# The block inverse of a chunked RWKV-7 mixer: both directions taken stage by stage, its copies on two engines

## The chip, the cores and the metric

One core of a Trainium2 chip runs the whole program. The metric is device time in microseconds (us) of one execution; a stated time is the median of several runs.

## The reference

One layer of a hybrid backbone over 256 latent and 256 context tokens, width 2048. The part that matters here is the bidirectional RWKV-7 mixer (16 heads of 64), beside the gates that the layer computes from the same projection:

```
def rwkv7_scan(s0, r, decay, k, v, kk, a, reverse):
    def step(S, inp):
        r_t, w_t, k_t, v_t, kk_t, a_t = inp
        sa = jnp.einsum('bhvk,bhk->bhv', S, kk_t)
        S = (S * w_t[:, :, None, :] - sa[..., None] * (kk_t * a_t)[:, :, None, :]
             + v_t[..., None] * k_t[:, :, None, :])
        return S, jnp.einsum('bhvk,bhk->bhv', S, r_t)
...
def merge_branches(p_gate, y_rwkv, y_diff, w_pa, w_pb, w_out):
    gates = jax.nn.sigmoid(p_gate.reshape(*p_gate.shape[:-1], 2, D_MODEL))
    mixed = gates[..., 0, :] * (y_rwkv @ w_pa) + gates[..., 1, :] * (y_diff @ w_pb)
    return mixed @ w_out
```

A mixture of experts (32 experts, two for each token) follows.

## The kernel before

The scan is done in chunks of 64 tokens: 8 chunks (4 of context, 4 of latent tokens) in each of two directions. Within a chunk the recurrence is a triangular system, so each chunk, direction and head needs the inverse of a 64x64 unit triangular matrix A. The heads are worked through in four quarters, q0 to q3, each with two head pairs (o = 0 and 1). For a quarter and head pair, A holds 2 directions x 8 chunks x 2 heads = 32 matrices; index m = 0 to 15 is the forward direction, 16 to 31 the backward one.

`inverse` works by blocks of 32. The two diagonal blocks of all 64 matrices of a quarter are inverted together on VectorE, row by row (L1426, L1428, 31 steps). Two transposes then give ZT (L1431) and Z (L1433). The off-diagonal block is completed by two 32x32 products for each matrix on TensorE: ph = A x ZT (L1442), evacuated into H, which is the same tile as ZT (L1444); then pz = H x Z (L1451), evacuated back into A (L1453). The inverted diagonal blocks are copied from Z into A as well (L1454). A head pair's operands lie in 64 partitions of its own, so the ph products of o = 0 and of o = 1 stand at two different positions of the engine's array (`tile_position`), each 32 rows by 32 columns; so do the pz products.

Behind it, `deltas` multiplies with the finished A: pW (L1243, alternating between the two head pairs, both into one PSUM bank) and pu (L1251, one head pair in each bank), four times, then pG (L1268), which alternates over head pairs and heads, four positions, with a bank for each head pair; then the chain of states pS.

The rest of the layer is a second stream of work: projections as products of 128x128 weights with 256 tokens (L490, the operands split into a high part whi by ScalarE, L968, and a low part wlo, L969, by VectorE, or by GpSimd for those parts that are recorded while an inverse is being recorded), and the sums of the conditioning vector's projection, ada (L614). In this part of the program these are mostly the gates' products. The generators of the mixer yield a number of microseconds; `interleave` then advances the second stream by that many, times 0.444. This gives the order in which instructions are recorded, which is their priority; a scheduler then places them on the engines by readiness and priority, and each engine runs its list in order.

Of the kernel before, what the change touches and what calls it, by code (L numbers as in the profile page):

```python
# [200 lines left out]
class Body:  # L201
# [1205 lines left out]
    def rows(self, o, i):  # L1407
        return slice((1 - o) * 64 + 32 * i, (1 - o) * 64 + 32 * i + 32)

    def inverse(self, As):  # L1410

        nc, tl, pst = self.nc, self.rwt, self.pst
        NB = 2 * NC * 2
        Av = [A.rearrange("p d c h t -> p (d c h) t") for A in As]

        na = tl("na", [P, 32, 32], tag="b0")
        z = tl("z", [P, 32, 32], tag="b1")
        prod = tl("prod", [P, 32, 32], tag="b2")
        rows = self.rows
        nc.vector.transpose(na.rearrange("b s t -> b t s"), self.dg16.rearrange("p d n t -> p t (d n)"))  # L1420
        yield 1.5
        nc.gpsimd.memset(z, 0.0)
        nc.gpsimd.memset(z.rearrange("b s t -> b (s t)")[:, ::33], 1.0)
        for s in range(30, -1, -1):
            n = 31 - s
            nc.vector.tensor_tensor(prod[:, :n, :n], z[:, s + 1:, s + 1:], na[:, s, s + 1:].unsqueeze(1).to_broadcast([P, n, n]),  # L1426
                                    ALU.mult)
            nc.vector.tensor_reduce(z[:, s + 1:, s], prod[:, :n, :n], AX.X, ALU.add)  # L1428
            yield 0.25 + n * n * 0.002
        ZT = H = tl("ZT", [P, NB, 32], tag="b3")  # L1430
        nc.vector.transpose(ZT.rearrange("p n s -> p s n"), z.rearrange("b t s -> b s t"))  # L1431
        Z = self.rb.tile([P, NB, 32], F32, tag="s", name="Z")
        nc.vector.transpose(Z.rearrange("p n t -> p t n"), z)  # L1433
        yield 3.077

        for g in range(2):
            ph = [pst("ph") for _ in range(2)]
            for o in range(2):
                r0, r1 = rows(o, 0), rows(o, 1)
                for n in range(16):  # L1440
                    m = g * 16 + n
                    nc.tensor.matmul(ph[o][r1, n * 32:n * 32 + 32], Av[o][r0, m, 32:64], ZT[r0, m, :],  # L1442
                                     start=True, stop=True, tile_position=(r0.start, r1.start))
                nc.scalar.copy(H[r1, g * 16:g * 16 + 16], ph[o][r1, :].rearrange("p (n t) -> p n t", n=16))  # L1444
            yield 0.7
            pz = [pst("pz") for _ in range(2)]
            for o in range(2):
                r0, r1 = rows(o, 0), rows(o, 1)
                for n in range(16):
                    m = g * 16 + n  # L1450
                    nc.tensor.matmul(pz[o][r0, n * 32:n * 32 + 32], H[r1, m, :], Z[r1, m, :],  # L1451
                                     start=True, stop=True, tile_position=(r1.start, r0.start))
                nc.scalar.copy(Av[o][r0, g * 16:g * 16 + 16, 32:64], pz[o][r0, :].rearrange("p (n t) -> p n t", n=16))  # L1453
                nc.scalar.copy(Av[o][rows(o, g), :, 32 * g:32 * g + 32], Z[rows(o, g)])  # L1454
            yield 0.7

    def pst(self, name):
        return self.ps.tile([P, 512], F32, tag="ps", name=name)
# [517 lines left out]
```

## Time and profile before

| | |
|---|---|
| median of 3 runs | 2495.0 us (2490.64, 2495.00, 2501.33) |
| the profiled execution | 2500.59 us, span 2499.0 us |
| mean granted TensorE clock | 0.971 of full speed |
| TensorE (PE) busy | 2337.1 us, 94% |
| VectorE (DVE) busy | 1203.3 us, 48% |
| ScalarE (ACT) busy | 796.1 us, 32% |
| GpSimd (POOL) busy | 218.5 us, 9% |
| the four quarters of the mixer | about 730 to 1340 us of the span |
| the experts | about 1600 us to the end, DMA share 0.99 |

The span is the time from the first to the last instruction of the profiled execution. A busy engine need not be a fast one: the granted clock says at which share of 2.4 GHz TensorE ran, 1.00 or 0.50 (1.2 GHz) at any moment, something between as a mean.

### The profile page before, as it was taken

The page shows a single profiled execution, that of the slowest core. Times are in us where ns is not written, and L with a number is a line of the kernel's source. Part 1 is how long each engine was busy: PE and PEld are TensorE (multiplying, and loading weights), DVE is VectorE, ACT ScalarE, POOL GpSimd, SP SyncE. Part 2 cuts the span into 40 slices and gives each one's busy share as a digit, 9 for nine tenths or more (in the row PEclk, how much of TensorE's full clock was granted, in tenths as well). Part 3 has the DMA queues.
Part 4 walks back from the last instruction along what each step waited for, and adds up shares of the span by engine and source line. Part 5 has one row for each costly group of instructions (what it writes and reads, how often), then busy time and mean ns, then how long its engine had stood idle before and what let it go on. Part 6 is the DMA issues. An engine that isn't in the chain of part 4 may idle for free.

```text
span 2499.0 us, 45067 instructions
## 1 busy us (share of the span) xinstructions
PE 2337.1 (94%) x18419; PEld 1647.7 (66%) x18419; DVE 1203.3 (48%) x2234; ACT 796.1 (32%) x1479; POOL 218.5 (9%) x279
## 2 busy tenths in 40 slices
PE   6999989899999999999999898999999999999997
PEld 3799987788998787787899877444334443343342
DVE  3355578768656574685755665222222222222223
ACT  3322345455345564565644343000000000000000
POOL 0110012112113332201000000000000000000000
PEclk9999999999998997999899999999999999999999
DMA  9977764557754242353347896899999999999997
GB/s 348 329 246 233 239 218 137 166 176 245 236 172 136 78 129 94 114 174 85 122 130 233 255 333 235 323 427 428 427 427 427 428 428 427 428 427 427 428 427 325
DMA packets 205476, 691.46 MB, mean 277 GB/s; under 512 B 31768, under 2 KB 69328, under 8 KB 179792
## 3 DMA queue, kind: packets, MB, share of 16 engines
q1 hardware_dynamic: 205264, 688.53, 73.8%
q8 instruction: 146, 2.39, 0.4%
q14 instruction: 66, 0.54, 0.1%
HBM read 666.66 MB, written 21.78 MB: 275 GB/s over the span
## 4 chain that ended last, share of the span: by engine, by line
PE 54%; DMA 17%; DVE 8%; issue 4%; ACT 3%; POOL 2%; SPq 0%; DVEq 0%; POOLq 0%; ACTq 0%
PE acc L490 12%; DMA xd<-in_exp_w_dram 10%; PE pa L1822 9%; PE po L1856 9%; PE pt L1754 5%; PE acc L815 4%; PE pt L1873 3%; DMA raw<-in_ws_dram 2%; DMA w<-in_exp_w_dram 2%; PE pc L1132 1%; DVE prod L1426 1%; PE pu L1251 1%; PE pz L1451 1%; PE ph L1442 1%; DVE wlo L969 1%
## 5 line engine op out<-in xcount | busy, mean ns | idle before, releaser
L968 ACT CAST whi<-raw 128x512 fp32r<-128x512 f32 (+1 forms) x463 | 280.2, 614 | 318.8 <-PE acc L490 144.5
L969 DVE TENSOR_TENSOR wlo<-raw,whi 128x512 fp32r<-128x512 f32 (+1 forms) x420 | 289.2, 702 | 89.5 <-ACT whi L968 83.5
L490 PE MATMUL acc<-xr,whi 128*128 128x256 f32 (+1 forms) x1248 | 273.4, 297 | 0.0
L490 PE MATMUL acc<-xd,whi 128*128 128x256 f32 (+1 forms) x1248 | 267.9, 292 | 0.7 <-ACT whi L968 0.7
L1822 PE MATMUL pa<-w,hg 128*64 128x512 f32 x1024 | 226.5, 594 | 16.2 <-DMA w<-in_exp_w_dram 12.8
L1856 PE MATMUL po<-w,hT 128*64 128x512 f32 (+1 forms) x1040 | 230.8, 590 | 1.5 <-DMA w<-in_exp_w_dram 0.7
L490 PEld LDWEIGHTS acc<-xr,whi 128*128 128x128 f32 (+1 forms) x1248 | 212.3, 198 | 19.6 <-issue 18.0
L490 PEld LDWEIGHTS acc<-xd,whi 128*128 128x128 f32 (+1 forms) x1248 | 207.2, 193 | 18.7 <-issue 13.6
L1769 DVE TENSOR_TENSOR hm<-hm,pa 128x512 f32<-128x512 f32 x16 | 11.0, 688 | 405.9 <-PE pa L1822 405.9
L490 PE MATMUL acc<-xr,wlo 128*128 128x256 f32 (+1 forms) x624 | 184.5, 296 | 4.7 <-DVE wlo L969 4.1
L490 PE MATMUL acc<-xd,wlo 128*128 128x256 f32 (+1 forms) x624 | 181.9, 291 | 1.1 <-DVE wlo L969 1.1
L607 DVE SCALAR_TENSOR_TENSOR ada<-raw,cs,ada 128x512 f32<-128x512 f32 x180 | 137.1, 769 | 95.2 <-DMA raw<-in_ws_dram 94.8
L1822 PEld LDWEIGHTS pa<-w,hg 128*64 128x64 f32 x1024 | 71.8, 137 | 165.6 <-issue 132.8
L1856 PEld LDWEIGHTS po<-w,hT 128*64 128x64 f32 x1040 | 70.4, 137 | 133.8 <-issue 127.3
L1880 DVE TENSOR_TENSOR acc<-acc,pt 128x512 f32<-128x512 f32 x112 | 75.3, 682 | 152.4 <-PE pt L1873 152.4
L1863 ACT ACTIVATE ohl<-po,gc 128x512 fp32r<-128x512 f32 x60 | 41.3, 688 | 296.6 <-PE po L1856 296.6
L490 PEld LDWEIGHTS acc<-xr,wlo 128*128 128x128 f32 (+1 forms) x624 | 123.6, 198 | 8.9 <-DVE wlo L969 5.7
L1754 PE MATMUL pt<-pe,xa 128*128 128x128 f32 x1024 | 123.6, 279 | 5.9 <-DVE hg L1756 5.2
L1822 PE MATMUL pa<-xd,hg 128*64 128x512 f32 x496 | 113.1, 598 | 16.1 <-DMA xd<-in_exp_w_dram 16.1
L1822 PE MATMUL pa<-xr,hg 128*64 128x512 f32 x496 | 113.1, 598 | 15.4 <-DMA xr<-in_exp_w_dram 15.4
L1754 PEld LDWEIGHTS pt<-pe,xa 128*128 128x128 f32 x1024 | 118.6, 194 | 12.1 <-DVE hg L1756 8.8
L490 PEld LDWEIGHTS acc<-xd,wlo 128*128 128x128 f32 (+1 forms) x624 | 120.3, 193 | 4.2 <-DVE wlo L969 1.5
(393 smaller groups left out, 4205.7 us busy)
## 6 DMA issues: line engine op xcount, KB each, us to landing
w<-in_exp_w_dram SPq DMA_DIRECT2D x128, 2048.0 KB
raw<-in_ws_dram SPq DMA_DIRECT2D x703, 256.0 KB
xr<-in_exp_w_dram SPq DMA_DIRECT2D x31, 2048.0 KB
xd<-in_exp_w_dram SPq DMA_DIRECT2D x31, 2048.0 KB
xt<-in_ws_dram SPq DMA_DIRECT2D x39, 512.0 KB
raw<-in_ws_dram SPq DMA_DIRECT2D x25, 512.0 KB
g<-gate SPq DMA_DIRECT2D x48, 128.0 KB
kvr<-own SPq DMA_DIRECT2D x16, 256.0 KB
```

The lines of the kernel that those rows point to most:

```text
L490: m = nc.tensor.matmul(acc[j][:M, n * T:n * T + T], a[:, k2, j * M:(j + 1) * M], (rl if i == 1 else rh)[k], start=(k == 0 and i == 0 and s ...
L607: nc.vector.scalar_tensor_tensor(a, raw, c, a, ALU.mult, ALU.add)
L815: nc.tensor.matmul(acc[i], a[:, i * P:(i + 1) * P], b[:, k - k0, :], start=(k == 0 and q == 0), stop=(k == KT - 1 and q == 2))
L968: self.nc.scalar.copy(hi, src)
L969: (eng or self.nc.vector).tensor_tensor(lo, src, f32(hi), ALU.subtract)
L1132: nc.tensor.matmul(pc[h][:, c * C:c * C + C], flat(kq[d][H2[h], c]), pr[d][H2[h], c], start=True, stop=True, tile_position=(h * 64, 0))
L1754: nc.tensor.matmul(p[:, k * P:(k + 1) * P], xa[:, i, (k4 + k) * P:(k4 + k + 1) * P], pe[:, i, :], start=(i == 0), stop=(i == 1))
L1822: nc.tensor.matmul(a[es_, :], hg[:, k4 + k, es_], w[:, e, k, :], start=(k4 + k == 0), stop=(k4 + k == KT - 1), tile_position=(0, e * 64))
L1856: nc.tensor.matmul(o[es_, :], hT[:, f, es_], w[:, e, f, hs], start=(f == 0), stop=(f == 3), tile_position=(0, e * 64))
L1863: nc.scalar.activation(oh[:, n, hs], o, AF.Copy, scale=gc)
L1873: nc.tensor.matmul(y, one[:, i * P:(i + 1) * P], o, start=(h == 0), stop=(h == 1))
L1880: nc.vector.tensor_tensor(acc[:, i, os], acc[:, i, os], y, ALU.add)
```

## The change

For each quarter, all copies of the diagonal blocks are recorded ahead of the products, half on ScalarE (o = 0) and half on VectorE (o = 1). Then ph is made for both directions (g = 0, 1) with the two head pairs alternating, each direction in a bank for both head pairs; then pz in the same way. The evacuations are split between the two engines like the copies. The yields become 6.0 and four times 1.4, where they were 3.077 and four times 0.7.

```diff
-        yield 3.077
-
+        yield 6.0
+
+        for o in range(2):
+            for i in range(2):
+                rs = rows(o, i)
+                (nc.vector.tensor_copy if o else nc.scalar.copy)(Av[o][rs, :, 32 * i:32 * i + 32], Z[rs])
+        ph = [pst("ph") for _ in range(2)]
         for g in range(2):
-            ph = [pst("ph") for _ in range(2)]
+            for n in range(16):
+                m = g * 16 + n
+                for o in range(2):
+                    r0, r1 = rows(o, 0), rows(o, 1)
+                    nc.tensor.matmul(ph[g][r1, n * 32:n * 32 + 32], Av[o][r0, m, 32:64], ZT[r0, m, :],
+                                     start=True, stop=True, tile_position=(r0.start, r1.start))
             for o in range(2):
-                r0, r1 = rows(o, 0), rows(o, 1)
-                for n in range(16):
-                    m = g * 16 + n
-                    nc.tensor.matmul(ph[o][r1, n * 32:n * 32 + 32], Av[o][r0, m, 32:64], ZT[r0, m, :],
-                                     start=True, stop=True, tile_position=(r0.start, r1.start))
-                nc.scalar.copy(H[r1, g * 16:g * 16 + 16], ph[o][r1, :].rearrange("p (n t) -> p n t", n=16))
-            yield 0.7
-            pz = [pst("pz") for _ in range(2)]
+                r1 = rows(o, 1)
+                (nc.vector.tensor_copy if o else nc.scalar.copy)(H[r1, g * 16:g * 16 + 16],
+                                                                 ph[g][r1, :].rearrange("p (n t) -> p n t", n=16))
+            yield 1.4
+        pz = [pst("pz") for _ in range(2)]
+        for g in range(2):
+            for n in range(16):
+                m = g * 16 + n
+                for o in range(2):
+                    r0, r1 = rows(o, 0), rows(o, 1)
+                    nc.tensor.matmul(pz[g][r0, n * 32:n * 32 + 32], H[r1, m, :], Z[r1, m, :],
+                                     start=True, stop=True, tile_position=(r1.start, r0.start))
             for o in range(2):
-                r0, r1 = rows(o, 0), rows(o, 1)
-                for n in range(16):
-                    m = g * 16 + n
-                    nc.tensor.matmul(pz[o][r0, n * 32:n * 32 + 32], H[r1, m, :], Z[r1, m, :],
-                                     start=True, stop=True, tile_position=(r1.start, r0.start))
-                nc.scalar.copy(Av[o][r0, g * 16:g * 16 + 16, 32:64], pz[o][r0, :].rearrange("p (n t) -> p n t", n=16))
-                nc.scalar.copy(Av[o][rows(o, g), :, 32 * g:32 * g + 32], Z[rows(o, g)])
-            yield 0.7
+                r0 = rows(o, 0)
+                (nc.vector.tensor_copy if o else nc.scalar.copy)(Av[o][r0, g * 16:g * 16 + 16, 32:64],
+                                                                 pz[g][r0, :].rearrange("p (n t) -> p n t", n=16))
+            yield 1.4
```

The scheduler's order shows what becomes of it on TensorE in q0, from the last gates' product ahead of ph. Here x32 counts 32 instructions in a row; xr, xd and whi, wlo are operands of the gates' products. Before:

```order
L490 MATMUL acc<-xr,wlo 128x256
L1442 MATMUL ph<-ZT,A 32x32 x32
L490 MATMUL acc<-xr,whi 128x256 x2
L490 MATMUL acc<-xr,wlo 128x256
L614 MATMUL ada<-raw,cs 32x256
L1451 MATMUL pz<-Z,ZT 32x32 x32
L1442 MATMUL ph<-ZT,A 32x32 x32
```

In the change, where ph stands in line 1446 and pz in line 1459:

```order
L490 MATMUL acc<-xr,wlo 128x256
L1446 MATMUL ph<-ZT,A 32x32 x64
L490 MATMUL acc<-xr,whi 128x256
L1459 MATMUL pz<-Z,ZT 32x32
L490 MATMUL acc<-xr,whi 128x256
L490 MATMUL acc<-xr,wlo 128x256
L614 MATMUL ada<-raw,cs 32x256 x2
```

The 64 ph instructions of both directions now follow each other; the gates' products ahead of them are as many as before, 2649 since the program's start.

The end of the same place in q0, on TensorE, from the last pz to the finished A's first uses pW and pu. Before:

```order
L1451 MATMUL pz<-Z,ZT 32x32 x16
L490 MATMUL acc<-xr,whi 128x256
L1451 MATMUL pz<-Z,ZT 32x32 x16
L1243 MATMUL pW<-W,A 64x64
L1251 MATMUL pu<-vu,A 64x64 x8
L490 MATMUL acc<-xr,whi 128x256
L490 MATMUL acc<-xr,wlo 128x256
```

In the change:

```order
L1459 MATMUL pz<-Z,ZT 32x32 x32
L490 MATMUL acc<-xr,wlo 128x256
L1459 MATMUL pz<-Z,ZT 32x32 x31
L1243 MATMUL pW<-W,A 64x64 x16
L1251 MATMUL pu<-vu,A 64x64 x16
L1243 MATMUL pW<-W,A 64x64 x16
L1251 MATMUL pu<-vu,A 64x64 x16
```

Before, a pW, eight pu and then 14 gates' products stood ahead of the other 15 pW; now pW and pu follow pz without products between. In q2 and q3 a pW, eight pu and two or three gates' products still stand ahead of the run.

VectorE in q0, from the last reduction of the inverse (L1428) to the first evacuations of pu and pW. Before:

```order
L1428 TENSOR_REDUCE z<-prod 128x31
L1431 STREAM_TRANSPOSE ZT<-z 128x32x32
L1433 STREAM_TRANSPOSE Z<-z 128x32x32
L1253 COPY vu<-pu 64x512
L1245 COPY W<-pW 128x512
L1253 COPY vu<-pu 64x512 x2
```

In the change, with a wlo of the second stream ahead of the transposes that stood some rows earlier before:

```order
L1428 TENSOR_REDUCE z<-prod 128x31
L969 TENSOR_TENSOR wlo<-raw,whi 128x512
L1431 STREAM_TRANSPOSE ZT<-z 128x32x32
L1433 STREAM_TRANSPOSE Z<-z 128x32x32
L1439 COPY A<-Z 32x32x32 x2
L1450 COPY ZT<-ph 32x512 x2
L1463 COPY A<-pz 32x16x32 x2
L1253 COPY vu<-pu 64x512
```

Six copies come in between the transposes and pu's; ScalarE loses as many.

## Rows read from the trace of the kernel before

**Rows 1.** The page, part 1: busy us, share of the span, instructions.

```profile
PE 2337.1 (94%) x18419; PEld 1647.7 (66%) x18419; DVE 1203.3 (48%) x2234; ACT 796.1 (32%) x1479; POOL 218.5 (9%) x279
```

**Rows 2.** Windows behind each inverse: busy us by engine, clock, DMA share, GB/s.

```profile
core 0: us, PE busy (x) PEld busy (x) DVE busy (x) ACT busy (x) POOL busy (x), PEclk, DMA share, GB/s
...
793.00:821.00 28.00, 27.75 (x342) 23.86 (x343) 2.57 (x3) 10.54 (x15) 4.25 (x4) 0.51 0.17 51
953.00:980.00 27.00, 26.11 (x328) 23.55 (x330) 4.07 (x4) 10.02 (x14) 2.96 (x3) 0.51 0.22 66
1112.00:1131.00 19.00, 19.00 (x312) 17.91 (x312) 4.71 (x8) 10.34 (x16) 0.00 (x0) 0.74 0.19 59
1271.00:1289.00 18.00, 18.00 (x316) 16.63 (x314) 6.58 (x10) 11.36 (x17) 0.31 (x1) 0.79 0.34 104
```

**Rows 3.** Timeline of TensorE, q0: start, duration, records, idle time before.

```profile
793.25 3.35 PE L1442 MATMUL ph<-ZT,A 32*32 32x32 f32 x64 [3.33 <-DVE ZT L1431]
796.53 0.80 PE L490 MATMUL acc<-xr,whi 128*128 128x256 f32 x2
...
813.18 1.91 PE L1251 MATMUL pu<-vu,A 64*64 64x64 f32 x16
...
817.66 1.07 PE L614 MATMUL ada<-raw,cs 128*32 128x256 f32 x4
...
819.60 1.60 PE L1243 MATMUL pW<-W,A 64*64 64x64 f32 x30
```

**Rows 4.** Timeline of TensorE, q1: the first ph and pW's run.

```profile
953.88 3.40 PE L1442 MATMUL ph<-ZT,A 32*32 32x32 f32 x64 [2.75 <-DVE ZT L1431]
...
978.92 1.97 PE L1243 MATMUL pW<-W,A 64*64 64x64 f32 x30
```

**Rows 5.** Timeline of TensorE, q2: the first ph and pW's run.

```profile
1112.51 2.11 PE L1442 MATMUL ph<-ZT,A 32*32 32x32 f32 x64
...
1131.39 1.14 PE L1243 MATMUL pW<-W,A 64*64 64x64 f32 x30
```

**Rows 6.** Timeline of TensorE, q3: products at either clock, ph, pW's run.

```profile
1270.74 0.40 PE L490 MATMUL acc<-xd,whi 128*128 128x256 f32 x2
...
1271.10 0.40 PE L490 MATMUL acc<-xd,whi 128*128 128x256 f32 x2
...
1271.55 2.11 PE L1442 MATMUL ph<-ZT,A 32*32 32x32 f32 x64
1273.59 0.50 PE L490 MATMUL acc<-xd,whi 128*128 128x256 f32 x2
...
1280.37 0.63 PE L490 MATMUL acc<-xd,whi 128*128 128x256 f32 x2
...
1281.01 0.60 PE L490 MATMUL acc<-xd,whi 128*128 128x256 f32 x2
...
1289.10 1.97 PE L1243 MATMUL pW<-W,A 64*64 64x64 f32 x30
```

**Rows 7.** Timeline of TensorE at full clock: products of 64x64 in deltas.

```profile
825.56 1.15 PE L1243 MATMUL pW<-W,A 64*64 64x64 f32 x32
826.54 1.85 PE L1251 MATMUL pu<-vu,A 64*64 64x64 f32 x32
828.32 1.13 PE L1054 MATMUL pw<-lw,w 96*128 96x512 f32 x2
...
1145.14 1.71 PE L1268 MATMUL pG<-kt,W 64*64 64x64 f32 x96
```

**Rows 8.** Timeline of TensorE between q2 and q3, without gates' products.

```profile
1195.14 6.25 PE L1132 MATMUL pc<-P,kq 64*128 64x64 f32 x64
...
1208.33 2.67 PE L1132 MATMUL pc<-P,kq 64*128 64x64 f32 x32
```

**Rows 9.** Timeline of ScalarE in q0 and of VectorE in q2: copies.

```profile
797.24 1.04 ACT L1454 COPY A<-Z 32x1024 f32<-32x1024 f32 x1
...
1128.27 0.69 DVE L1253 COPY vu<-pu 64x512 f32<-64x512 f32 x1 [13.47 <-PE pu L1251]
```

**Rows 10.** Groups of GpSimd: count, busy us, mean ns, idle before.

```profile
L969 POOL TENSOR_TENSOR wlo<-raw,whi 128x512 fp32r<-128x512 f32 x43 | 63.3, 1489 | 113.0 <-ACT whi L968 109.2 <-PE acc L490 2.8 <-PE ada L614 1.0
```

## The prediction

> **What bounds the kernel now.** I read the page's busy times first, then windows for the granted clock, then the timeline of the three engines around each inverse. TensorE is busy for 94% of the span [rows 1] and its program order is fixed, so time goes where TensorE waits or runs slowly. At the end of each of the four inverses (one per quarter, q0 to q3) the reader is to see the second: in the 27 to 28 us behind the inverse's last transposes the granted clock is 0.51 in q0 and q1, which is the 1.2 GHz level nearly throughout, and 0.74 and 0.79 in q2 and q3 [rows 2]. In q0 and q1 TensorE had waited before it, 3.33 and 2.75 us for ZT [rows 3, 4]; in q2 and q3 it did not wait and the clock still fell: the means say 10 of 19 and 8 of 18 us at the low level.
>
> Measured from the first ph to the run of thirty pW records, the four ends take 819.60 - 793.25 = 26.35, 25.04, 18.88 and 17.55 us [rows 3 to 6], 88 us together. That is what the change rewrites; the 32x32 products (256 records a quarter, two for each instruction), the gates' products put between them and the clock are its three terms.
>
> **The pace of small products.** A record of ph costs (796.53 - 793.25) / 64 = 51.3 ns at 1.2 GHz [rows 3] and (1273.59 - 1271.55) / 64 = 31.9 ns at 2.4 GHz [rows 6]. In before, 16 instructions in a row go to one position of the array; the change alternates between two. No row has alternating 32x32 products, so the price is bounded by the same pair of cases at 64x64: pu keeps one position and costs (828.32 - 826.54) / 32 = 55.6 ns, pW alternates between two and costs (826.54 - 825.56) / 32 = 30.6 ns [rows 7]. Lower bound of the gain: nothing, 51.3 and 31.9 stay. Upper: the ratio of pW to pu, 0.55, giving 28.2 and 17.5 ns. I take the upper one, since the two rows differ in the alternation alone; pG, which alternates between four positions, shows that records can follow each other within 1.71 us / 96 = 17.8 ns.
>
> There is a rule against it. In before the two head pairs write to a bank each (ph[0], ph[1]); in the change both write into ph[g]. The Trainium skill, page "TensorEngine Tiling (Array Packing)", section "Restrictions and Gotchas", says that different row tiles cannot access the same PSUM bank at the same time. The trace disagrees for 64x64: pW's two row positions fill one bank, at 30.6 ns. By the rule the pace would stay as before, which is rival A. The Trainium skill's page "TensorE: Matmul & The Clock Gate" (Part 1, on small matmuls) also gives a floor of about 25 ns from start to start; by that the two quarters at full clock would gain 256 x 7.5 ns = 1.9 us less each. The row of pG speaks against it.
>
> **The sum by quarters.** A gates' product costs 0.12 us at 2.4 GHz (three from 1270.74 to 1271.10) and 0.213 at 1.2 (three from 1280.37 to 1281.01) [rows 6]; the ada pair about 1.0 at 1.2 GHz [rows 3], so 0.5 at full. Counted in the two orders, between first ph and pW's run stand 30, 30, 34 and 30 products before and 12, 19, 16 and 20 after. The 57 that drop out come later at 0.12 each. The diff's larger yields ask for more products; the scheduler places fewer here, because the chain is ready sooner.
>
> q0, clock low as before: 256 x 28.2 ns = 7.2, 12 products 2.6, ada 1.0, together 10.8 us. Before: 26.35 less 2.1 for the pW pair and pu that stand ahead of the run [rows 3] = 24.2. Gain 13.4, less 18 later products (2.2) and two ada (0.5): 10.7.
> q1: 7.2 + 19 x 0.213 + 1.0 = 12.3 against 25.04 - 2.1 = 22.9; less 1.3: 9.3.
> q2, clock full at its start: 256 x 17.5 ns = 4.5, 16 products 1.9, ada 0.5, pW pair and pu 0.95, together 7.85 against 18.88; less 2.2 for products, plus 0.25 for ada: 9.1.
> q3: 4.5 + 2.4 + 0.5 + 0.95 = 8.35 against 17.55; less 1.2 and 0.25: 7.8.
> Sum 37 us, before the clock behind it.
>
> **The clock behind it.** Before, the products stood between pz and pW's run, and the clock came back about there: in q0 pz is over at 813, and the run at 819.60 takes 1.60 us for 30 records where 32 take 1.15 at full [rows 3, 7], so it stayed low about 7 us behind pz. After, pW and pu follow pz directly. How long the clock then stays low is unknown. Nearest rows: those 7 us; and the stretch from 1195.14, where pc, px and transposes ran with no gates' products in between: low for over 13 us, until within the pc at 1208.33 (64 records took 6.25 us at 1195.14, so 32 would take 3.1 at the low clock; these took 2.67) [rows 8]. I take 10 us, as pW's stream is like neither. Ten us at half speed lose 5; about 0.5 was lost in pW's run before too. So 4.5 each in q0 and q1. In q2 and q3 the run of 19 and 18 us began at the full clock and lost it on the way [rows 2]; the new run is about 8 us with a block of full products in its middle, so I call a fall an even chance: 1.5 us in the run and 5 behind it, half of that, 3.25 each. Together 15.5.
>
> **What is moved on other engines.** Twenty-four copies go from ScalarE to VectorE, six a quarter. ScalarE's copy of Z takes 1.04 us; VectorE's of the same length has no row, and lies between half of its 512-element copy (0.69 us) and twice it, and VectorE stood idle for 13.47 us here [rows 9]. They delay pz only if H is late: ZT is followed by 1.9 us for Z, two copies of Z and one of H, some 4 to 5.4 us, while TensorE has ph and 10 or more products, 4 us or more. Nothing to 1 us a quarter; I take 0.5, so 2. Queued behind them on VectorE are only pu's copies, later than pz. Also, "lo" subtractions made while an inverse is emitted go to GpSimd: 48 instead of 43. At 1.49 us each [rows 10] against 0.69 they cost at most 5 x 0.8 = 4 us where a product waits, nothing where the four ready parts cover it; I take nothing. The waits of 3.33 and 2.75 us stay: up to the first ph the order holds 2649 products in both, and in q1 as many in between as before within one.
>
> Net: 37 - 15.5 - 2 = 19.5 us. Nothing later takes it back: products moved to the end of the stage are counted, and the expert stage starts when the earlier one ends. The profiled execution took 2500.6 us, 5.6 over the median; I put the gain on the median: 2495 - 20 = 2475 us.
>
> **Rivals.**
> A, alternating gains nothing (a shared bank, or one position's pace is the engine's): then 2 x 5.9 us in q0 and q1, 2 x 3.7 in q2 and q3, and the fall certain there (6.5 more): the gain is gone, about 2500. For it the rule above; against it pW. Chance 0.10.
> B, the clock stays high in q2 and q3 and returns within 7 us in q0 and q1: 30 to 35 us, about 2463. For it the denser pattern. 0.17.
> C, in q0 and q1 the clock stays low through all of pW, pu and pG. These take 1145.14 + 1.71 - 1131.39 = 15.5 us at full [rows 5, 7], so 15.5 lost each, not 4.5: 2497. For it the 13 us of [rows 8]; against it that this stream holds pk and pw, 512 columns wide. 0.13.
> D, slower: the same in all four quarters, 62 us lost against 37 won: 2522. It decides where the low stretch behind pz passes 18 us in every quarter (4 x 18 / 2 = 36). Against it: q2 and q3 enter with a full clock. 0.06.
> The forecast, 13 to 30 us: 0.54.
>
> **How the numbers follow.** Half a per cent, 12.5 us, is about what a measurement of this kernel tells from no change. Faster by more: the forecast and B, 0.54 + 0.17 = 0.71. Within: C and most of A, 0.20. Slower: D and the far side of A, 0.09. The range runs from B's best, 2458, to C, 2497; outside lie D, the worst of A and a sliver below. The forecast's own range is 2465 to 2482.
>
> **What would show it.** ph's 128 records in about 3.6 us in q0 and 2.2 in q3: right; 6.5 and 4: A. The first ph to pW's run: about 11, 12, 8, 8 us. The granted clock behind pz: back within 7, 10 or 16 us tells B, forecast and C apart. The waits for ZT stay near 3 us; if they go, I read the order wrongly. TensorE waiting for H for over 1 us means that the copies were mis-sized. The most likely way to be wrong is the clock.

## The result, and the profile after

The changed kernel took 2468.5 us (median of 5 runs, 2462.95 to 2478.11) against 2495.0 us beside it: ratio 0.9897, 95% interval 0.9873 to 0.9920, so 26.5 us or 1.1% faster. Run a second time, beside other kernels, it took 2464.75 us against 2497.9: 0.9871 (0.9826 to 0.9915). The profiled execution took 2462.95 us, 37.6 under the profiled one of before; the first is the shortest of its kernel's runs and the second among the longest of its own, so that the medians tell the gain better.

The page of the changed kernel, part 1, answers to [rows 1]; TensorE is busy 41.8 us less.

```profile
PE 2295.3 (93%) x18419; PEld 1607.1 (65%) x18419; DVE 1221.5 (50%) x2253; ACT 779.2 (32%) x1455; POOL 228.6 (9%) x284
```

Windows of the same lengths behind each inverse, to be held against [rows 2] (busy us by engine, then the granted clock):

```profile
788.50:816.50 28.00, 25.82 (x671) 21.53 (x671) 17.29 (x26) 16.16 (x25) 4.75 (x6) 1.00 0.27 79
934.50:961.50 27.00, 25.25 (x548) 21.17 (x548) 14.03 (x20) 13.85 (x22) 2.55 (x2) 0.87 0.27 79
1091.00:1110.00 19.00, 19.00 (x478) 15.99 (x476) 12.81 (x18) 9.65 (x15) 0.00 (x0) 1.00 0.43 137
1235.00:1253.00 18.00, 18.00 (x515) 16.46 (x514) 11.95 (x19) 11.27 (x20) 0.31 (x1) 1.00 0.48 141
```

The clock column is the surprise: 0.51, 0.51, 0.74, 0.79 before, now 1.00, 0.87, 1.00, 1.00. TensorE also does twice as many records in the window of q0 (671 for 342). Its timeline at the four ends, which answers to [rows 3 to 6]:

```profile
788.88 2.21 PE L1446 MATMUL ph<-ZT,A 32*32 32x32 f32 x128 [1.06 <-DVE ZT L1431]
...
793.64 1.20 PE L1459 MATMUL pz<-Z,ZT 32*32 32x32 f32 x64
...
796.21 0.68 PE L1243 MATMUL pW<-W,A 64*64 64x64 f32 x14
...
934.92 2.23 PE L1446 MATMUL ph<-ZT,A 32*32 32x32 f32 x115 [3.15 <-DVE ZT L1431]
...
946.76 1.15 PE L1243 MATMUL pW<-W,A 64*64 64x64 f32 x32
...
1091.58 2.21 PE L1446 MATMUL ph<-ZT,A 32*32 32x32 f32 x128
...
1101.02 1.14 PE L1243 MATMUL pW<-W,A 64*64 64x64 f32 x30
...
1235.42 2.21 PE L1446 MATMUL ph<-ZT,A 32*32 32x32 f32 x128
...
1245.13 1.14 PE L1243 MATMUL pW<-W,A 64*64 64x64 f32 x30
```

128 records of ph take 2.21 us, 17.3 ns each, where 64 took 2.11 [rows 5, 6]. From the first ph to pW's run it is 7.3, 11.8, 9.4 and 9.7 us, 38 us together for 88. The wait for ZT in q0 is 1.06 us, no longer 3.33.

Part of this is given back at the seams behind q0 and q1. A seam is the stretch between two quarters in which TensorE does pcf, pc, px and transposes of the next quarter, with few or no gates' products between. TensorE's timeline there, and for one other wait:

```profile
864.15 0.39 PE L490 MATMUL acc<-xr,wlo 128*128 128x256 f32 x1 [3.97 <-POOL wlo L969]
...
865.88 7.09 PE L1132 MATMUL pc<-P,kq 64*128 64x64 f32 x64
...
1005.58 0.37 PE L1295 MATMUL py<-zb 1*128 1x512 bf16 x1 [2.15 <-ACT y L1358]
...
1013.49 0.39 PE L490 MATMUL acc<-xr,wlo 128*128 128x256 f32 x1 [2.47 <-POOL wlo L969]
```

GpSimd's timeline at the first of them:

```profile
858.84 1.24 POOL L1084 TENSOR_TENSOR bon<-bon,f 128x256 f32<-128x256 f32 x1 [1.07 <-ACT f L1079]
860.15 1.59 POOL L1085 TENSOR_TENSOR f<-f,k 128x512 f32<-128x512 f32 x1
861.71 0.72 POOL L1103 TENSOR_TENSOR bon<-bon,k 128x256 f32<-128x256 f32 x1
862.39 4.80 POOL L969 TENSOR_TENSOR wlo<-raw,whi 128x512 fp32r<-128x512 f32 x3
```

Windows behind the two waits:

```profile
864.00:878.00 14.00, 13.85 (x111) 13.08 (x112) 6.28 (x9) 2.98 (x5) 3.19 (x3) 0.53 0.39 130
1014.00:1028.00 14.00, 14.00 (x115) 13.55 (x115) 6.19 (x9) 3.81 (x7) 1.45 (x1) 0.53 0.36 112
```

At these two places five of the 48 subtractions that GpSimd now does (43 before) stand in its list behind the feature work of the next quarter (f x k, bon x k, lines 1084 to 1103): the three shown, and two at the second seam. A gates' product waits 3.97 us for one of them, another 2.47, and behind both the clock is 0.53 for 14 us, through pc's stretch. That is not wholly new: before, the seam behind q2 showed the same, 1.76 us of waiting and then the pc rows at half clock [rows 8]. In the changed kernel that seam is clean: 64 records of pc take 3.79 us there. So one seam of three lost the clock before, and two do after. TensorE's timeline at the seam behind q2, before and then in the change:

```profile
1194.51 0.70 PE L1107 MATMUL pcf<-bon,cst 128*128 128x256 f32 x2 [1.76 <-DVE bon L1104]
...
1165.16 3.79 PE L1132 MATMUL pc<-P,kq 64*128 64x64 f32 x64
```

### The profile page after: what moved, and what is told of

It reads as the page before. It is cut to its first block, busy times and chain, and to the rows that moved or that the text cites. A ratio compares the mean times of both kernels' runs of the same rounds, so it can differ in the third digit from the quotient of the medians.

```text
span 2461.1 us, 45031 instructions
## 1 busy us (share of the span) xinstructions
PE 2295.3 (93%) x18419; PEld 1607.1 (65%) x18419; DVE 1221.5 (50%) x2253; ACT 779.2 (32%) x1455; POOL 228.6 (9%) x284
## 4 chain that ended last, share of the span: by engine, by line
PE 61%; DMA 20%; DVE 8%; issue 4%; ACT 3%; POOL 2%; SPq 1%; DVEq 0%; POOLq 0%; ACTq 0%
PE acc L490 14%; DMA xd<-in_exp_w_dram 10%; PE pa L1832 9%; PE po L1866 9%; PE pt L1764 5%; PE acc L521 5%; DMA raw<-in_ws_dram 5%; PE pt L1883 3%; PE acc L815 3%; DMA w<-in_exp_w_dram 2%; PE pc L1132 1%; DVE wlo L969 1%; PE ada L651 1%; PE pu L1251 1%; PE ada L614 1%
## 5 line engine op out<-in xcount | busy, mean ns | idle before, releaser
L490 PE MATMUL acc<-xr,whi 128*128 128x256 f32 (+1 forms) x1248 | 265.4, 289 | 0.9 <-DVE g L754 0.9
L1832 PE MATMUL pa<-w,hg 128*64 128x512 f32 x1024 | 226.3, 594 | 14.8 <-DMA w<-in_exp_w_dram 11.7
L490 PEld LDWEIGHTS acc<-xr,whi 128*128 128x128 f32 (+1 forms) x1248 | 204.5, 190 | 17.4 <-issue 12.8
L490 PE MATMUL acc<-xr,wlo 128*128 128x256 f32 (+1 forms) x624 | 178.9, 287 | 6.9 <-POOL wlo L969 6.9
L490 PEld LDWEIGHTS acc<-xr,wlo 128*128 128x128 f32 (+1 forms) x624 | 118.6, 190 | 10.7 <-POOL wlo L969 7.8
```

Of the source, the lines that this page charges most:

```text
L490: m = nc.tensor.matmul(acc[j][:M, n * T:n * T + T], a[:, k2, j * M:(j + 1) * M], (rl if i == 1 else rh)[k], start=(k == 0 and i == 0 and s ...
L1832: nc.tensor.matmul(a[es_, :], hg[:, k4 + k, es_], w[:, e, k, :], start=(k4 + k == 0), stop=(k4 + k == KT - 1), tile_position=(0, e * 64))
```

## The experiments

Three theories were told apart. **Theory 1**: alternating the two positions pays. **Theory 2**: recording both directions together, with other yields and fewer products between, pays. **Theory G**: the subtractions on GpSimd take part of the gain back.

**The alternation alone, put into the kernel before.** For ph, and in the same way for pz:

```diff
-            for o in range(2):
-                r0, r1 = rows(o, 0), rows(o, 1)
-                for n in range(16):
-                    m = g * 16 + n
+            for n in range(16):
+                m = g * 16 + n
+                for o in range(2):
+                    r0, r1 = rows(o, 0), rows(o, 1)
                     nc.tensor.matmul(ph[o][r1, n * 32:n * 32 + 32], Av[o][r0, m, 32:64], ZT[r0, m, :],
...
+            for o in range(2):
+                r1 = rows(o, 1)
                 nc.scalar.copy(H[r1, g * 16:g * 16 + 16], ph[o][r1, :].rearrange("p (n t) -> p n t", n=16))
```

> The kernel before, with one edit: the ph and pz products of the two head pairs alternate within a direction; each head pair keeps a bank of its own, the copies stay on ScalarE behind each direction, the yields stay. Theory 1 (the alternation itself is the gain, in shared or own banks): ph at about 17 ns a record at full clock and 28 at half, where before had 31.9 and 51.3; 256 records a quarter, so about 6 us less in q0 and q1, 4 in q2 and q3, 20 in all, and more if the clock no longer falls: 2465 to 2480 us. Theory 2 (the alternation is not what pays; recording both directions together and fewer products in between do): the pace stays at 32 and 51 ns, 2490 to 2500 us. Bank theory (two row positions into one bank cost): own banks run faster than the 16.8 ns a record that the changed kernel shows with shared ones.

Measured: 2475.7 us, ratio 0.9923 (0.9899 to 0.9947), about 19 us faster. Its TensorE timeline in q0 and q3:

```profile
787.95 1.20 PE L1442 MATMUL ph<-ZT,A 32*32 32x32 f32 x64 [3.33 <-DVE ZT L1431]
...
790.74 1.91 PE L1453 MATMUL pz<-Z,ZT 32*32 32x32 f32 x32
...
795.79 1.74 PE L1442 MATMUL ph<-ZT,A 32*32 32x32 f32 x58
...
810.78 1.14 PE L1243 MATMUL pW<-W,A 64*64 64x64 f32 x30
...
1256.19 1.21 PE L1442 MATMUL ph<-ZT,A 32*32 32x32 f32 x59
```

Theory 1 holds for the pace: 64 records of ph with a bank for each head pair take 1.20 us, the same as 64 of pz in a shared bank in the changed kernel (793.64). So the bank theory falls, for two positions that write to different partitions of the bank, as they do here. But pz is not alternating here: its operand H comes by two copies of ScalarE in turn, and the scheduler places 32 records of one head pair as soon as they are ready (1.91 us for 32 in q0). The clock still falls in all four ends; q0 needs 810.78 - 787.95 = 22.8 us to pW's run. Most of the change's gain is here already; the change's 0.9897 and this 0.9923 have intervals of 0.0024 to either side that overlap, so it is not shown that the full change is faster than the alternation alone.

**The changed kernel without the alternation** (the loop over o outside the loop over n again, for ph and pz; everything else of the change stays).

> The changed kernel, with the two head pairs' products no longer alternating: 16 in a row at one position, then 16 at the other; banks, copies and yields as in the change. Theory 1: ph back at 32 ns a record at full clock, 256 x 15 ns = 3.9 us more a quarter, 16 in all, and if the clock falls in the longer run up to 10 more a quarter: 2480 to 2505 us, granted clock below 0.9 behind ph in at least two quarters. Theory 2: time and clock as in the change, 2463 to 2475 us.

Measured: 2504.2 us, 1.0038 (1.0018 to 1.0058): all the rest of the change by itself makes the kernel slower, by 9 us. TensorE's timeline in q0 and q2:

```profile
784.89 4.62 PE L1446 MATMUL ph<-ZT,A 32*32 32x32 f32 x128 [1.06 <-DVE ZT L1431]
...
1117.62 3.93 PE L1446 MATMUL ph<-ZT,A 32*32 32x32 f32 x128
...
1121.80 1.72 PE L1459 MATMUL pz<-Z,ZT 32*32 32x32 f32 x32
...
1127.51 4.95 PE L1459 MATMUL pz<-Z,ZT 32*32 32x32 f32 x96
```

The four windows behind its inverses:

```profile
784.50:812.50 28.00, 27.61 (x463) 25.14 (x463) 8.76 (x12) 8.45 (x13) 1.84 (x2) 0.63 0.16 50
949.00:976.00 27.00, 26.49 (x446) 24.89 (x447) 9.63 (x14) 9.73 (x16) 2.54 (x2) 0.64 0.19 56
1117.00:1136.00 19.00, 19.00 (x309) 17.19 (x310) 9.44 (x14) 5.53 (x8) 0.00 (x0) 0.63 0.32 99
1274.00:1292.00 18.00, 18.00 (x299) 16.19 (x298) 7.35 (x12) 7.62 (x14) 0.31 (x1) 0.64 0.32 101
```

In q2 TensorE had not waited. ph's rows of 16 ran at the full clock (3.93 us for 128, 30.7 ns each), and the clock fell right behind them: the first 32 of pz take 1.72 us, and the other 96 take 51.6 ns a record. With the alternation the same place stays at 1.00. In q2 and q3 the alternation thus decides the clock as well as the pace.

**Only pz not alternating** in the changed kernel, to size the two.

> The changed kernel with only pz no longer alternating (ph still does). Theory P (the alternation pays by its pace alone): 128 records a quarter at 31 instead of 17 ns, 1.8 us a quarter, 7 us in all: 2473 to 2480 us. Theory K (it also keeps the granted clock full through the ends; the run without any alternation lost it in all four quarters, and the run with ph alternating and pz in rows lost it too): the clock falls in the pz rows or behind, 3 to 7 us more a quarter: 2485 to 2500 us.

Measured: 2482.5 us, 0.9951 (0.9927 to 0.9975), some 14 to 20 us over the change by the two ratios of that, where the pace alone accounts for 7. Timeline in q2 and q3:

```profile
1108.96 2.21 PE L1446 MATMUL ph<-ZT,A 32*32 32x32 f32 x128
...
1111.41 1.19 PE L1459 MATMUL pz<-Z,ZT 32*32 32x32 f32 x32
...
1120.68 1.97 PE L1243 MATMUL pW<-W,A 64*64 64x64 f32 x30
...
1266.18 3.02 PE L1459 MATMUL pz<-Z,ZT 32*32 32x32 f32 x96
...
1270.87 1.14 PE L1243 MATMUL pW<-W,A 64*64 64x64 f32 x30
```

In q2 the clock fell behind pz's rows (pW's run 1.97 us); in q3 it did not (1.14). In q0 and q1 the windows show 0.70 and 0.64 for the 1.00 and 0.87 of the change. The median lies midway between the two theories' ranges, 2473 to 2480 and 2485 to 2500 us. Of the 14 to 20 us the pace explains 7; that the lost clock is the rest, about as much again or more, is the likeliest reading, but no run takes the two apart.

**The yields alone, in the kernel before** (6.0 and 1.4 for 3.077 and 0.7).

> The kernel before, with the larger yields alone (6.0 and 1.4 where it has 3.077 and 0.7): more of the gates' products are recorded ahead of and between the inverse's products, and more subtractions fall to GpSimd. Theory 1: no gain, the ends of the quarters get longer by the products put between, the same number less later: 2490 to 2505 us. Theory 2 (the products put ahead cover the waits for ZT): the waits of 3.33 and 2.75 us for ZT shrink to about 1, the clock behind them stays full, 2470 to 2485 us.

Measured: 2498.7 us, 1.001 (0.9989 to 1.0032): no gain. The wait for ZT in q0 did shrink, to 1.04 us, as theory 2 said; but the clock fell all the same, behind ph's first 64 records, which still ran at the full clock, and in the pz rows of 16 that follow (TensorE's timeline in q0):

```profile
783.95 2.08 PE L1442 MATMUL ph<-ZT,A 32*32 32x32 f32 x64 [1.04 <-DVE ZT L1431]
...
787.05 3.19 PE L1451 MATMUL pz<-Z,ZT 32*32 32x32 f32 x61
```

**The yields of before, in the changed kernel.**

> The changed kernel with the yields of before (3.077 and 0.7): alternation, both directions together and the copies on two engines stay, 43 instead of 48 subtractions go to GpSimd. Theory G (the larger yields bring the late subtractions on GpSimd at the ends of q0 and q1, and those waits of 3.97 and 2.47 us with the half clock behind them cost up to 19 us): the waits go, 2450 to 2460 us. Rival (the larger yields are what covers ZT and keeps the clock full at the inverse): the waits for ZT are back at 3.3 and 2.8 us, the clock falls behind ph in q0 and q1, 2470 to 2485 us.

Measured: 2462.2 us, 0.9869 (0.9844 to 0.9894), the same as the change. Both theories are half right: the waits for GpSimd at the seams are gone, and the waits for ZT are back, 3.35 us in q0 and 4.46 in q1, with the clock at half behind them. TensorE's timeline in q0 and at the seam behind it, and three windows:

```profile
787.65 3.63 PE L1446 MATMUL ph<-ZT,A 32*32 32x32 f32 x128 [3.35 <-DVE ZT L1431]
...
799.89 1.97 PE L1243 MATMUL pW<-W,A 64*64 64x64 f32 x32
...
871.45 0.70 PE L1107 MATMUL pcf<-bon,cst 128*128 128x256 f32 x2 [2.18 <-DVE bon L1104]
...
800.00:807.00 7.00, 7.00 (x106) 7.00 (x106) 1.73 (x3) 1.74 (x3) 0.00 (x0) 0.50 0.01 2
807.00:815.00 8.00, 8.00 (x138) 6.35 (x139) 3.30 (x6) 4.04 (x7) 0.00 (x0) 0.97 0.08 18
872.00:886.00 14.00, 14.00 (x115) 13.47 (x114) 4.79 (x8) 4.21 (x7) 0.00 (x0) 0.51 0.33 110
```

The larger yields take 2.3 us off the wait for ZT in q0, and the time stays the same. The seams are no cleaner without them: TensorE waits there for bon instead of wlo (2.18 us behind q0, 1.44 behind q1), and the clock is lost behind both all the same. The first rows also give the alternating pace at half clock: 3.63 us / 128 = 28.4 ns.

**The late subtractions on VectorE.** In the changed kernel, behind the last row of the inverse:

```diff
+        self.low = None
         yield 6.0
```

> The changed kernel, with the subtractions for wlo put back on VectorE for what is recorded behind the last row of the inverse (those recorded during its rows stay on GpSimd). Theory G (the waits for GpSimd's wlo of 3.97 and 2.47 us at the ends of q0 and q1, and the half clock of about 13 us that follows each, cost 6.4 + 13 = 19 us): both waits and both low stretches go, 2448 to 2456 us. Rival H (another operand is late in the same place, or VectorE's transposes come later by the subtractions that it gets, 0.7 us each): the low stretches stay, or the first ph comes later by as much; 2462 to 2472 us.

Measured: 2458.9 us, 0.9840 (0.9804 to 0.9876). The same kernel was run again beside the change on one chip.

> The changed kernel again, beside the three below on one chip. All theories: 2463 to 2475 us; TensorE waits about 4.0 and 2.2 to 2.5 us for GpSimd's wlo at the seams behind q0 and q1, with the clock at half behind both.

> The changed kernel with the late subtractions on VectorE, again, on the same chip. Theory G (GpSimd's late wlo cost at least their waits, 6.4 us, and less than the 19 us first thought, as the first such run waited 2.43 us for bon and lost the clock at the same seam): 6 to 14 us under the change. Rival (chance between chips and executions): within 4 us of it.

Measured: the change 2464.75 us (mean of its six 2466.2), this one 2457.0 (mean 2456.2), 0.9836 (0.9791 to 0.9882): 7.8 us less by the medians, 10 by the means. With spreads of 6.3 and 5.5 us in six runs each, the means' difference is uncertain by some 7.5: theory G in the smaller size fits, and the rival (within 4 us) is not quite out by this pair alone; the first run leans the same way (0.9840 against 0.9897). The two waits for wlo are gone. In q0 the first ph waits 2.10 us for ZT instead of 1.06, as rival H said, and in q1 1.38 instead of 3.15. But the seams are not clean; TensorE's timeline behind q0:

```profile
862.92 1.22 PE L1107 MATMUL pcf<-bon,cst 128*128 128x256 f32 x2 [2.45 <-DVE bon L1104]
864.07 7.09 PE L1132 MATMUL pc<-P,kq 64*128 64x64 f32 x64
```

and the windows behind that wait and at the seam behind q2:

```profile
862.00:889.00 27.00, 26.08 (x185) 22.43 (x186) 10.02 (x18) 8.18 (x15) 1.10 (x2) 0.51 0.17 54
1161.00:1178.00 17.00, 16.34 (x146) 15.55 (x146) 7.21 (x13) 4.79 (x8) 1.10 (x2) 0.60 0.37 122
```

TensorE now waits 2.45 us for bon behind q0, the next thing late, and the clock is at half for 27 us instead of 14. The seam behind q1 is clean (1.00), but the one behind q2, clean in the change, loses the clock. So this run gives the price of the subtractions' place as a whole; that the two waits for wlo are what loses the clock at the seams is not shown. Taking the wait away would need bon earlier as well, which the next run tried.

**bon's products recorded ahead of f x k and kq**, on top of that.

```diff
                 nc.gpsimd.tensor_tensor(fsum, fsum, f[:, T:], ALU.add)
+                nc.gpsimd.tensor_tensor(fsum, fsum, k[:, T:], ALU.mult)
+                nc.vector.scalar_tensor_tensor(fsum, r, col(V["rk"]), fsum, ALU.mult, ALU.mult)
...
-        nc.gpsimd.tensor_tensor(fsum, fsum, k[:, T:], ALU.mult)
-        nc.vector.scalar_tensor_tensor(fsum, r, col(V["rk"]), fsum, ALU.mult, ALU.mult)
```

> The run with the late subtractions on VectorE, and one more edit: the product bon x k (GpSimd) and r x bon (VectorE) are recorded as soon as their operand is there, ahead of f x k and kq instead of behind them, so that pcf, which TensorE waits for at each seam between quarters, is ready earlier. In that run TensorE waited 1.66, 2.43, 1.67 and 1.47 us for it, and behind the second and the fourth the clock was half for about 28 and 13 us. Theory S (the wait at the seam is what costs the clock there): the waits go under 1 us, the clock stays full, 15 to 20 us less than that run, 2438 to 2446 us. Rival (pc then waits for kq at the same place, or the stretch of pc, px and pq loses the clock by itself): 2452 to 2462 us.

Measured: 2464.9 us, 0.9873 (0.9850 to 0.9896), no better than without it. The edit did not do what it was meant to: pcf's waits for bon are 10.8 us in six cases, more than the 7.2 in four of the run before, and the scheduler placed pcf and other instructions elsewhere too. Whether the seams would keep the clock without their waits stays open.

**All copies on ScalarE**, in the changed kernel, twice, and together with the subtractions on VectorE.

> The changed kernel with all its copies and evacuations on ScalarE as before. Four copies of Z of 1.04 us each and two evacuations of 0.58 stand in a row there before pz's operand is whole. Theory C (the split over two engines matters): TensorE waits for H ahead of pz by up to 2 us a quarter, and the clock may fall there; 2475 to 2490 us. Rival (the gates' products between ph and pz cover it, as they do 2 to 3 us in the change): as the change, 2463 to 2473 us.

> The changed kernel with all copies on ScalarE, again, on the same chip. Theory C2 (the split is no gain: six copies a quarter on VectorE stand ahead of other work there, and the ends are longer without it but hidden by gates' products): 8 to 14 us under the change, as in the first run of it. Rival (its first run differed by chip or by which seams lost the clock): within 4 us of the change.

> The changed kernel with both edits: all copies on ScalarE, late subtractions on VectorE. If the two are separate costs of the change they add: 14 to 24 us under it, 2445 to 2452 us. If both only take away the same waits for GpSimd's wlo at the seams, no more than either alone: 2453 to 2460 us.

Measured: 2455.7 us, 0.9844 (0.9821 to 0.9866) the first time, which looked like a gain over the change; beside the change on one chip 2462.05 us, 0.9864 (0.9819 to 0.9909), 2.7 us under it, well inside the spread. Both edits together 2460.2 us, 0.9851 (0.9808 to 0.9893): they don't add. Neither theory C (slower without the split) nor C2 (8 to 14 us faster) holds: the split of the copies over two engines is worth nothing that can be measured here. Without it the end of q0 is longer (11.7 us for 7.3), but filled with gates' products that have to be done in any case. TensorE does not wait for wlo at the seams in these runs either, and in the second of them it waits 3.82 us for bon behind q0 instead.

## Why the prediction was right, step by step

It said 2475 us by a gain of 20; 26.5 were measured, within its own 13 to 30. The mechanism held, the pace of alternating products; the sum was near for a good part by luck: wrong terms went against each other.

**The pace: right.** Forecast 17.5 and 28.2 ns; measured 17.3 (2.21 / 128) and 28.4. Rival A is out: two row positions in one bank run as fast as in two banks. The prediction took pW and pu to differ in the alternation alone; they differ in their banks too, and only the run with the alternation alone settles which of the two it was. The rule of the Trainium skill, page "TensorEngine Tiling (Array Packing)", section "Restrictions and Gotchas", which spoke for rival A, does not show here, for 32x32 any more than for 64x64. The floor of about 25 ns that the Trainium skill's page "TensorE: Matmul & The Clock Gate", Part 1, gives is passed too, at 17.3 ns.

**The ends: right in sum only.** Forecast 10.8, 12.3, 7.85 and 8.35 us, 39.3 together; measured 7.3, 11.8, 9.4 and 9.7, 38.2. The products between were counted rightly (12, 19, 16 and 20). q0 is shorter because its clock was full, where the prediction took half. q2 and q3 are 1.6 and 1.4 us longer than forecast, in part because ada stands there twice, about 0.55 us each, where 0.5 was taken in all.

**The clock behind the ends: mis-sized.** The prediction took 15.5 us: low for 10 us behind pz in q0 and q1, an even chance of a fall in q2 and q3. In the profile of the change nothing is low behind pz, in any quarter. In that of its second run q1 was, for 6 to 7 us (pz ends at 951.2; windows):

```profile
937.00:958.00 21.00, 20.63 (x386) 18.70 (x387) 8.34 (x13) 7.41 (x12) 2.54 (x2) 0.51 0.25 83
958.00:964.00 6.00, 6.00 (x92) 4.36 (x90) 2.59 (x4) 2.94 (x5) 0.00 (x0) 1.00 0.00 0
```

So the term is 0 to 3.5 us: on this point rival B was the true course. For q2 and q3 the run without alternation shows what kept the clock: with rows of 16 it fell there without any wait ahead. In q0 the clock was never low in the change; with the old yields, where it fell ahead of ph, it stayed low for 7 us behind pz (800 to 807), not 10. (By its own 30 to 35 us B's best is 2460 us, not 2458; nothing hangs on it.)

**"The waits of 3.33 and 2.75 us stay": wrong for q0.** It is 1.06 us with the new yields, 3.35 with the old ones in the same kernel, and 1.04 with the new yields in the kernel before. That as many products stand ahead of ph was not enough to tell; by which step the yields shorten it, the runs don't show. In q1 it stayed, at 3.15, and there the clock did fall.

**The copies: right, and smaller.** 2 us were taken; TensorE waited 0.8 us for H in all. VectorE's copy of Z takes 0.68 us, in the range given.

**GpSimd: the step that failed.** "I take nothing", with a bound of 4 us: the prediction priced five subtractions by their own length, and trusted four ready parts to cover them. They cost by their place, behind 3.5 us of feature work in GpSimd's list: waits of 3.97 and 2.47 us, 6.4 together. Their price is about 8 us by the medians of the run that moves them, uncertain by nearly as much, as other waits take their place.

**"Nothing later takes it back": near enough.** From pW's run in q3 to the end of the span it took 2499.0 - 1289.10 = 1209.9 us before and 2461.1 - 1245.13 = 1216.0 in the change. By count of TensorE's records 39 of the 57 products that dropped out stand there now, 4.7 us at 0.12 each, which the sum had taken off.

With the measured terms the sum is 37 - (0 to 3.5) - 0.8 - 7.8 = 25 to 28 us. The stretches from pW's run to the next quarter's first ph, seam included, fit the 7.8, but only in sum: 134.3, 133.6 and 140.2 us before, 138.7, 144.8 and 134.4 in the change, with none, 8 and 11 products more in them. At 0.12 us each, an estimate, that is 14.6 us lost in the two stretches whose seam lost the clock, and 7.1 won behind q2, where the seam became clean. That win was not forecast, why it came was not tested, and it is the luck in the sum.

## What to carry to other kernels

Small products that follow each other at one position of the array are worth alternating between positions, in one bank or several, and the scheduler must be kept from undoing it: where the operands of both positions don't become ready together, it puts the rows back. Read what it gains from the granted clock as well as from the pace. When work is moved onto a lightly used engine, look at what stands ahead of it in that engine's list at the moment it is needed; its own length tells only a part of the price. And a wait that is taken away can be followed by the next one at the same place: at the seams bon was late where wlo no longer was.

## What the runs showed of the hardware that was not expected

The order of positions alone changed the granted clock. At q2, with no wait of TensorE ahead, 16 products in a row at one position lost it (0.63 over 19 us in the changed kernel without alternation), alternating ones kept it (1.00), with nearly the same gates' products among them (17 and 16).

The same program differs between executions by which stretches lose the clock: q1's window of 27 us reads 0.87 in one profile of the change; in the other it is 0.51 for 21 us and 1.00 for the next 6. Those executions took 2462.95 and 2474.28 us, with mean granted clocks of 0.983 and 0.977; the kernel before had 0.971, and the change without alternation 0.966.

A wait's length did not by itself tell whether the clock falls. In the change it stayed at 1.00 behind a wait of 2.15 us (1005.58, for y), where gates' products followed, and fell behind 2.47 and 3.97; before, it fell behind 1.76 [rows 8], at a seam where none followed.
